# A hybrid decoder block on one core: first branch projection over eight banks, six more slabs in seven products, a shorter recurrence on VectorE

## The chip, the cores and the metric

The kernel runs on one core of a Trainium2 chip. What counts is the device time of one execution in microseconds. A NeuronCore has TensorE (PE in the profile, its weight loads PEld), VectorE (DVE), ScalarE (ACT), GpSimd (POOL) and SyncE (SP), which issues most of the loads. Each engine works through its own queue in order; the engines wait for each other by semaphores. TensorE writes into PSUM, eight banks of 128 x 512 float32 numbers here.

## The reference

One block of a decoder on 512 tokens of width 1024, with 16 meta tokens ahead (T = 528), in float32. Cut to what matters here:

```python
u = rmsnorm(h, mix_norm_w)
q, k, v, g_ret, lru_in, lru_gate, gate_a, gate_b = split(u @ w_in)      # eight times 1024 columns
o = chunk_retention(rotary(q), rotary(k) * dk ** -0.5, v)               # 8 heads, chunks of 128
y_ret = (silu(g_ret) * headnorm(o)) @ w_branch_ret
c = causal_depthwise_conv(lru_in, conv_w, conv_b)                       # 4 taps
r = sigmoid(c @ wa + ba); i = sigmoid(c @ wx + bx)                      # 4 blocks of 256
log_a = -8 * r * softplus(-lam); a = exp(log_a)
h_t = a_t * h_{t-1} + sqrt(-expm1(2 * log_a)) * (i * c)                 # the recurrence
y_lru = (gelu(lru_gate) * hs) @ w_branch_lru
h = h + (sigmoid(gate_a) * y_ret + sigmoid(gate_b) * y_lru) @ w_out
h = h + swiglu(rmsnorm(h, ffn_norm_w))                                  # hidden 2816
return rmsnorm(h, final_norm_w)[:, 16:]
```

## The kernel before

**Products.** Every float32 operand is split in two parts, `hi` (rounded to float32r by ScalarE, line 358) and `lo` (the rest, by VectorE, line 364). A product is three matmuls: hi x hi, hi x lo, lo x hi. The text counts matmuls as products where it counts TensorE's instructions.

**Slabs.** `w_in` is worked in 32 slabs of 256 columns, by their first letters: Q, K, G (retention), I (`lru_in`), L (`lru_gate`), A (`gate_a`), B (`gate_b`), four of each. A slab's weight is a 2 x 2 matrix of quarters (`a11`, `a12`, `a21`, `a22`, each 128 x 512), multiplied with the 2 x 2 matrix of blocks of u (`b11` to `b22`, 512 rows and 256 tokens, 264 with half the meta tokens). *Plain* (`plain`, `plain512`) it takes eight block products of twelve matmuls, 96. *Fast* (`fast`, `fast512`, `fast528`) it is Strassen's scheme in Winograd's form: seven block products, 84 matmuls. That needs sums of quarters (`s1` to `s4`, made by `combine` on VectorE, line 283, or for a next fast slab's `s1` by an accumulating load on GpSimd's queue), the differences `t1` to `t4` of u's blocks, held in the dictionary U, and a longer eviction: `pz`, `ws`, `u2` collect partial sums of four banks or half banks z, w, y, x, and two additions write the result. `plain_slab` says which slabs are plain: K0, G0, I2, I3, all L and all B; the gates of A and most of Q, K, G, I0 and I1 are fast.

**Pieces and their ring.** `emit` makes the pieces in the order of `pieces`, which follows PLAN: load a quarter, combine if needed, cast, subtract. A plain slab has four pieces of 128 x 512, a fast one seven. `hi` and `lo` have nine buffers each (RING), the raw quarters eight, the sums three.

**Steps.** PLAN lists the steps: R0 to R3 (queries, keys, values, retention gates; the heads' work is dealt out in small pieces behind later products by `defer` and `tick`), A (sigmoid gates of the first branch), I (`lru_in` and the convolution), BR (`branch`: `w_branch_ret`, two halves of four banks, each half running over all eight row tiles of 128; a source's split parts are held from the first half to the second), T (the recurrent gates of a block and, deferred, `recurrence`), L (`lru_gate`), B, BL (second branch, `branch` too, with `merged`). The step BR gives back the buffers of t1 to t4 first, BL those of the four blocks.

**Recurrence.** With t = tanh(4 softplus r) and e = exp(-8 softplus r) from ScalarE, six instructions a half block on VectorE and one on GpSimd: d = (e + 1) t, d = (e - 1) + d, d = (e + 1) d, a = -d / 2 + e, u = (a + 1) sqrt(t), GpSimd's product with i c (line 1241), the scan. GpSimd also makes i c itself (line 1215, 128 x 1056).

**Order.** The queues are not in the written order: except for the first steps, a scheduler with a timeline of its own sorts the instructions of each engine when the program is built. It lets TensorE change between open accumulations where a piece or a bank comes late. Work buffers come from 32 slots of 128 x 1056 float32 (`Slots`).

Of the kernel before, what the change touches and what calls it, by code (L numbers as in the profile page):

```python
# [17 lines left out]
P = 128  # L18
D = 1024
# [48 lines left out]
FIRST_LOADS = "w1 w2 w3 x1 w4 w5 w6 w7 r2 m r3 r0 r1"  # L68


PLAN = "R0 R1 R2 R3 A0 A1 A2 A3 I0 I1 BR T0 L0 I2 T1 L1 I3 L2 T2 B0 L3 T3 B1 B2 B3 BL"

PLAIN_R = "K0 G0".split()
NORM, LAST_NORM = 2.0, 3.7
SUM = 2.0

# [39 lines left out]
class Slots:  # L116
# [12 lines left out]
    def get(self, n=SEQ, dt=F32):  # L129
        if n <= T and dt == F32:  # L130
            if self.halves:
                slot, i = self.halves.pop(0)
            else:
                slot, i = [*self.open(dt), 0], 0
                self.halves.append((slot, 1))
            slot[2] += 1
            t = slot[1][:, i * T:i * T + n]
            self.held[id(t)] = (t, slot, i)
        else:
            tag, mem = self.open(dt)  # L140
            t = mem[:, :n]
            self.held[id(t)] = (t, tag, None)
        return t

    def put(self, *tiles):
        for t in tiles:
            _, slot, i = self.held.pop(id(t))
            if i is None:
                self.free.append(slot)
                continue  # L150
            slot[2] -= 1
            self.halves.append((slot, i))
# [6 lines left out]
def hybrid_block(ctx: ExitStack, tc: tile.TileContext, a: dict):  # L159
# [10 lines left out]
    def bank(name):  # L170
        return ps.tile([P, 512], F32, tag="ps", name=name)
# [48 lines left out]

    def plain_slab(key, i):
        if key == "w_in":
            return i in [{"Q": Q, "K": K, "G": G}[r[0]] + int(r[1]) for r in PLAIN_R] or LI + 2 <= i < GA or i >= GB
        return key == "w_fi" and i < FIRST

    pieces = []
    for n, (key, i) in enumerate(order):
        if n == 0:
            pieces += PLAIN_V
        if key in ("w_br", "w_bl"):  # L230

            pieces += [(key, k // 2, k % 2 + 2 * (1 - i)) for k in range(KT)]
        elif plain_slab(key, i):
            pieces += [(key, i, c) for c in PLAIN]
        elif key == "w_v":
            pieces += [(key, j, c) for c in FAST for j in (i, i + 1)] if i else []
        elif key in ("w_in", "w_fi"):
            pieces += [(key, i, c) for c in FAST]
        elif key == "w_fo":
            pass  # L240
        else:
            pieces += [(key, i, c) for c in range(2 if key == "gates" else 4)]
# [153 lines left out]
    def lookup(*args, **kw):  # L396
        state["table"] = behind(nc.scalar.activation(*args, **kw), state.get("table"))
# [39 lines left out]
    def mm3(out, wh, wl, xh, xl, start, stop):  # L437

        nc.tensor.matmul(out, wh, xh, start=start, stop=False, skip_group_check=True)  # L439
        nc.tensor.matmul(out, wh, xl, start=False, stop=False, skip_group_check=True)  # L440
        nc.tensor.matmul(out, wl, xh, start=False, stop=stop, skip_group_check=True)  # L441
        tick(3 * out.shape[-1] / 2400)
# [766 lines left out]
    def recurrence(group):  # L1209
        two = lambda t: t.rearrange("p (j t) -> p j t", j=2)  # L1210


        A = {}
        for b, r, g, c in group:
            nc.gpsimd.tensor_tensor(g, g, c, op=ALU.mult)
            put(c)
            A[b] = get(2 * T)
            a3, r3 = two(A[b]), two(r)
            for j in range(2):
                k = 2 * b + j  # L1220
                lookup(a3[:, j], r3[:, j], AF.Exp, scale=spm8[:, k:k + 1])
                lookup(r3[:, j], r3[:, j], AF.Tanh, scale=sp4[:, k:k + 1])
        yield STEPS[0]
        ds = {}
        for b, r, g, c in group:
            for j in range(2):
                a, t = two(A[b])[:, j], two(r)[:, j]
                d = ds[b, j] = get(T)
                nc.vector.scalar_tensor_tensor(d, a, 1.0, t, ALU.add, ALU.mult)
                lookup(t, t, AF.Sqrt)  # L1230
                nc.vector.scalar_tensor_tensor(d, a, 1.0, d, ALU.subtract, ALU.add)
            yield STEPS[1]
        for b, r, g, c in group:
            for j in range(2):
                a, t, d, g1 = two(A[b])[:, j], two(r)[:, j], ds[b, j], two(g)[:, j]
                nc.vector.scalar_tensor_tensor(d, a, 1.0, d, ALU.add, ALU.mult)
                nc.vector.scalar_tensor_tensor(a, d, -0.5, a, ALU.mult, ALU.add)
                put(d)
                yield STEPS[2]
                nc.vector.scalar_tensor_tensor(t, a, 1.0, t, ALU.add, ALU.mult)  # L1240
                nc.gpsimd.tensor_tensor(g1, g1, t, op=ALU.mult)
                yield STEPS[3]
                nc.vector.tensor_tensor_scan(t, a, g1, 0.0, ALU.mult, ALU.add)
            put(A[b], g)
            while Z[b] is None:
                yield 0.5
            z3 = two(Z[b])
            (nc.gpsimd if Z_POOL else nc.vector).tensor_tensor(z3, z3, two(r)[:, :, NM:], op=ALU.mult)
            put(r)
            ready.add(b)  # L1250

    def lru_gate(s):
        x = get(D)
        for j, pb in enumerate(plain512(LG + s, "lg")):
            lookup(x[:, j * SEQ:(j + 1) * SEQ], pb, AF.Gelu_apprx_tanh)
        Z[s] = x


# [22 lines left out]
    for step in plan:  # L1281
        s = int(step[1]) if step[1:2].isdigit() else None
        if step[0] == "R":
            ret_project(s)
            if s == 0:
                softplus()
            if s == 3:
                put(ropef)
        elif step == "BR":
            for i in range(4):  # L1290
                retained(i)
            for b in ("t1", "t2", "t3", "t4"):
                put(*U.pop(b))
            branch("w_br", lambda i: R[i], gated(macc, GA))
        elif step == "BL":
            for b in ("b11", "b12", "b21", "b22"):
                put(*U.pop(b))
            branch("w_bl", recurred, merged)
        elif step[0] == "A":
            gate(s, GA)  # L1300
        elif step[0] == "B":
            gate(s, GB)
        else:
            {"I": lru_in, "T": lru_gates, "L": lru_gate}[step[0]](*(int(i) for i in step[1:]))
# [325 lines left out]
```

## Time and profile before

| what | us |
|---|---|
| median of three runs | 901.25 (900.97 to 901.37) |
| the profiled execution's own time | 901.45 |
| its span, first to last instruction | 899.7 |
| VectorE busy in the span | 709.8 |
| ScalarE busy in the span | 500.2 |
| GpSimd busy in the span | 118.7 |

The profile gives, for one execution, every instruction with its start, duration and what ended its engine's wait. By the first matmuls of each step: the A gates start at 207.3 us, I0 and I1 fill about 260 to 288 with the first products of BR among them, BR ends at 328.9, T0 to B3 run from there to 466.5, BL to 510.7, the output projection to about 558, the FFN's first product to 787 and its second to the end. A matmul's recorded duration includes its way through the array, so the durations of neighbours overlap, and the distance between starts is what one costs. The granted TensorE clock is 0.998 of full speed over the span.

### The profile page before, as it was taken

The numbers are of one execution on the slowest core, as the hardware profiler recorded it, in microseconds if no ns is written. First come the engines' busy times: TensorE is split into PE (matmuls) and PEld (weight loads), VectorE is DVE, ScalarE is ACT, GpSimd is POOL, SyncE is SP. The second block draws the span as 40 slices with busy tenths as digits, with TensorE's granted clock in tenths as the row PEclk, the third lists the DMA queues.
The fourth block names the chain that finished last, engine by engine and source line by source line (L and its number), as shares of the span: only waits on it lengthen the run. The fifth ranks groups of instructions, "written<-read, shape, count | busy, mean of one in ns | idle before, by whom it ended". The sixth has DMA issues, their size and how long they took to land.

```text
span 899.7 us, 17038 instructions
## 1 busy us (share of the span) xinstructions
PE 888.5 (99%) x6470; PEld 841.4 (94%) x6470; DVE 709.8 (79%) x1164; ACT 500.2 (56%) x938; POOL 118.7 (13%) x154
## 2 busy tenths in 40 slices
PE   8999999999999999999999999999999999999996
PEld 7999999999999889999998888999999999988885
DVE  5998897999788738868745526989989998899973
ACT  6655655656556246857833315555556555665653
POOL 3202311212110011211200211000000000111112
PEclk9999999999999999999999999999999999999999
DMA  9734244445354333233442232133333335685622
GB/s 321 210 126 107 72 138 124 115 135 135 87 151 140 105 95 94 71 115 97 142 137 88 92 93 70 61 106 116 99 117 94 116 101 146 179 234 141 141 47 93
DMA packets 58145, 109.11 MB, mean 121 GB/s; under 512 B 6592, under 2 KB 6848, under 8 KB 58064
## 3 DMA queue, kind: packets, MB, share of 16 engines
q1 hardware_dynamic: 51152, 94.37, 33.0%
q0 software_dynamic: 5328, 9.70, 6.7%
q10 hardware_dynamic: 1584, 3.97, 1.4%
q8 instruction: 50, 0.82, 0.4%
q14 instruction: 31, 0.25, 0.1%
HBM read 105.92 MB, written 2.10 MB: 120 GB/s over the span
## 4 chain that ended last, share of the span: by engine, by line
PE 97%; DVE 1%; DMA 1%; ACT 1%; issue 0%; POOL 0%; POOLq 0%; ACTq 0%; DVEq 0%
PE zwf L449 4%; PE zwf L451 4%; PE zwf L450 4%; PE fo L441 4%; PE fo L440 4%; PE fo L439 4%; PE yxf L450 3%; PE yxf L449 3%; PE yxf L451 3%; PE gate L451 2%; PE lg L451 2%; PE lg L450 2%; PE gate L449 2%; PE gate L450 2%; PE lg L449 2%; PE wo L441 2%
## 5 line engine op out<-in xcount | busy, mean ns | idle before, releaser
L364 DVE TENSOR_TENSOR lo<-raw_w_in,hi 128x512 fp32r<-128x512 f32 x96 | 68.3, 718 | 28.5 <-ACT hi L358 26.3
L451 PE MATMUL zwf<-b,lo 128*128 128x256 f32 x320 | 90.2, 282 | 0.0
L449 PE MATMUL zwf<-b,hi 128*128 128x256 f32 x320 | 90.0, 282 | 0.0
L450 PE MATMUL zwf<-b,hi 128*128 128x256 f32 x320 | 90.0, 281 | 0.0
L358 ACT CAST hi<-raw_w_in 128x512 fp32r<-128x512 f32 x96 | 59.0, 620 | 50.0 <-PE w_br L440 13.9
L358 ACT CAST hi<-s_w_fi 128x512 fp32r<-128x512 f32 x80 | 49.7, 621 | 50.8 <-PE zwf L450 36.7
L450 PE MATMUL yxf<-b,hi 128*128 128x256 f32 x240 | 67.5, 281 | 0.0
L449 PE MATMUL yxf<-b,hi 128*128 128x256 f32 x240 | 67.4, 281 | 0.0
L451 PE MATMUL yxf<-b,lo 128*128 128x256 f32 x240 | 66.6, 281 | 0.0
L364 DVE TENSOR_TENSOR lo<-s_w_fi,hi 128x512 fp32r<-128x512 f32 x80 | 54.9, 687 | 13.5 <-ACT hi L358 13.5
L358 ACT CAST hi<-s_w_in 128x512 fp32r<-128x512 f32 x64 | 39.7, 623 | 42.7 <-PE zwgate L450 9.2
L358 ACT CAST hi<-raw_w_fi 128x512 fp32r<-128x512 f32 x68 | 41.9, 621 | 34.6 <-PE yxf L450 19.4
L450 PEld LDWEIGHTS zwf<-b,hi 128*128 128x128 f32 x320 | 60.6, 189 | 0.0
L449 PEld LDWEIGHTS zwf<-b,hi 128*128 128x128 f32 x320 | 60.5, 189 | 0.0
L451 PEld LDWEIGHTS zwf<-b,lo 128*128 128x128 f32 x320 | 60.5, 189 | 0.0
L440 PE MATMUL fo<-lo,b 128*128 128x512 f32 x158 | 59.1, 394 | 0.0
L439 PE MATMUL fo<-hi,b 128*128 128x512 f32 x158 | 57.5, 393 | 0.0
L441 PE MATMUL fo<-hi,b 128*128 128x512 f32 x158 | 56.1, 394 | 0.0
L505 ACT CAST b<-b 128x512 fp32r<-128x512 f32 (+3 forms) x58 | 39.2, 689 | 26.7 <-DVE b L1176 11.6
L506 DVE TENSOR_TENSOR b<-b,b 128x512 fp32r<-128x512 f32 (+3 forms) x58 | 48.7, 849 | 3.4 <-ACT b L505 3.3
L364 DVE TENSOR_TENSOR lo<-s_w_in,hi 128x512 fp32r<-128x512 f32 x64 | 43.5, 685 | 7.7 <-ACT hi L358 7.2
L364 DVE TENSOR_TENSOR lo<-raw_w_fi,hi 128x512 fp32r<-128x512 f32 x68 | 46.4, 685 | 3.9 <-ACT hi L358 3.3
(438 smaller groups left out, 3182.8 us busy)
## 6 DMA issues: line engine op xcount, KB each, us to landing
raw_w_in<-in_w_in SPq DMA_DIRECT2D x112, 256.0 KB, 3.2
raw_w_fi<-in_w_fi SPq DMA_DIRECT2D x86, 256.0 KB, 3.1
raw_w_fo<-in_w_fo SPq DMA_DIRECT2D x44, 256.0 KB, 4.0
raw_w_br<-in_w_br SPq DMA_DIRECT2D x16, 256.0 KB, 3.1
raw_w_bl<-in_w_bl SPq DMA_DIRECT2D x16, 256.0 KB, 3.5
raw_w_out<-in_w_out SPq DMA_DIRECT2D x16, 256.0 KB, 2.9
raw_w_v<-in_w_v SPq DMA_DIRECT2D x15, 256.0 KB, 5.5
s_w_in<-in_w_in SPq DMA_DIRECT2D x15, 256.0 KB, 3.4
```

Source lines behind the costliest of these rows:

```text
L358: highs.append(nc.scalar.copy(hi, src))
L364: return engine.tensor_tensor(lo, src, hi.bitcast(F32), op=ALU.subtract)
L439: nc.tensor.matmul(out, wh, xh, start=start, stop=False, skip_group_check=True)
L440: nc.tensor.matmul(out, wh, xl, start=False, stop=False, skip_group_check=True)
L441: nc.tensor.matmul(out, wl, xh, start=False, stop=stop, skip_group_check=True)
L449: nc.tensor.matmul(out, wh, xh, start=start and i == 0, stop=False, skip_group_check=True)
L450: nc.tensor.matmul(out, wh, xl, start=False, stop=False, skip_group_check=True)
L451: nc.tensor.matmul(out, wl, xh, start=False, stop=i == 3, skip_group_check=True)
L505: high = nc.scalar.copy(hi, src)
L506: low = engine.tensor_tensor(lo, src, hi.bitcast(F32), op=ALU.subtract)
```

## The change

Five edits.

1. **BR in eight banks.** `whole_branch` opens all eight banks of `w_br` and runs once over the eight row tiles. Each source R[i] (two tiles) is split, used for both halves at once, and its parts are given back; for the last source the products are grouped by bank, so that bank after bank is finished and evicted.
2. **PLAN.** BR stands ahead of I1, T2 ahead of L2, B0 behind T3.
3. **Fast slabs.** I2, L1 and B0 to B3 become fast; plain are I3, L0, L2, L3 (and K0, G0). `lru_gate` gets the fast path.
4. **Differences kept.** t1 to t4 stay in U until BL.
5. **Recurrence.** a = 1 - d with d = (e + 1) t takes the place of three instructions, and the two products on GpSimd (i c, and that with u) are made on VectorE. Per half block VectorE now has d, a, u, the product and the scan.

```diff
-PLAN = "R0 R1 R2 R3 A0 A1 A2 A3 I0 I1 BR T0 L0 I2 T1 L1 I3 L2 T2 B0 L3 T3 B1 B2 B3 BL"
+PLAN = "R0 R1 R2 R3 A0 A1 A2 A3 I0 BR I1 T0 L0 I2 T1 L1 I3 T2 L2 L3 T3 B0 B1 B2 B3 BL"
+PLAIN_L = "I3 L0 L2 L3".split()
...
-            return i in [{"Q": Q, "K": K, "G": G}[r[0]] + int(r[1]) for r in PLAIN_R] or LI + 2 <= i < GA or i >= GB
+            first = {"Q": Q, "K": K, "G": G, "I": LI, "L": LG, "B": GB}
+            return i in [first[r[0]] + int(r[1]) for r in PLAIN_R + PLAIN_L]
...
+        if key == "w_br":
+            pieces += [(key, k // 2, k % 2 + 2 * (1 - hf)) for k in range(KT) for hf in range(2)] if i == 0 else []
...
+    def whole_branch(key, source, done):
+        parts = {}
+        acc = [bank(f"{key}{c}") for c in range(KT)]
+        def product(c, k, w):
+            x = [p[:, k % 2 * SEQ:(k % 2 + 1) * SEQ] for p in parts[k // 2]]
+            mm3(acc[c], *(p[:, c % 4 * P:(c % 4 + 1) * P] for p in w), *x, k == 0, k == KT - 1)
+        for i in range(4):
+            f = source(i)
+            parts[i] = get(D, F32R), get(D, F32R)
+            split(parts[i], f)
+            put(f)
...
+            if i < 3:
+                for k, hf in names:
+                    w = weights(pieces_of[k, hf])[0]
+                    for c in range(4):
+                        product(4 * hf + c, k, w)
+            else:
+                ws = dict(zip(names, weights(*pieces_of.values())))
+                for c in range(KT):
+                    for k in (2 * i, 2 * i + 1):
+                        product(c, k, ws[k, c // 4])
+                    done(c, acc[c])
+            put(*parts.pop(i))
...
-            nc.gpsimd.tensor_tensor(g, g, c, op=ALU.mult)
+            nc.vector.tensor_tensor(g, g, c, op=ALU.mult)
...
                 nc.vector.scalar_tensor_tensor(d, a, 1.0, t, ALU.add, ALU.mult)
                 lookup(t, t, AF.Sqrt)
-                nc.vector.scalar_tensor_tensor(d, a, 1.0, d, ALU.subtract, ALU.add)
+                nc.vector.tensor_scalar(a, d, -1.0, 1.0, ALU.mult, ALU.add)
...
-                nc.vector.scalar_tensor_tensor(d, a, 1.0, d, ALU.add, ALU.mult)
-                nc.vector.scalar_tensor_tensor(a, d, -0.5, a, ALU.mult, ALU.add)
...
                 nc.vector.scalar_tensor_tensor(t, a, 1.0, t, ALU.add, ALU.mult)
-                nc.gpsimd.tensor_tensor(g1, g1, t, op=ALU.mult)
+                nc.vector.tensor_tensor(g1, g1, t, op=ALU.mult)
...
-            for b in ("t1", "t2", "t3", "t4"):
-                put(*U.pop(b))
-            branch("w_br", lambda i: R[i], gated(macc, GA))
+            whole_branch("w_br", lambda i: R[i], gated(macc, GA))
...
-            for b in ("b11", "b12", "b21", "b22"):
+            for b in list(U):
```

What the scheduler makes of it shows at three places; a name's last number is that of its buffer, and lines of the changed kernel are three higher for the same helper (442 for 439, 452 for 449, 367 for 364). On TensorE, the start of BR before: the last matmuls of I1's seventh product (`xli17`), then one bank after another of the first half (`w_br0_0`, `w_br0_1`).

```order
L449 MATMUL xli17_3851<-b7_113,hi138_3751 128x264
L450 MATMUL xli17_3851<-b8_114,hi138_3751 128x264
L451 MATMUL xli17_3851<-b7_113,lo138_3752 128x264
L439 MATMUL w_br0_0_4008<-b90_4012,hi142_3822 128x512
L440 MATMUL w_br0_0_4008<-b91_4013,hi142_3822 128x512
L441 MATMUL w_br0_0_4008<-b90_4012,lo142_3823 128x512
L439 MATMUL w_br0_1_4009<-b90_4012,hi142_3822 128x512
```

The start of BR in the change, a few matmuls behind I0's last: `w_br0` to `w_br7` are the eight banks, `hi137` and `hi138` are the weights of the second row tile (columns 0 to 511 and 512 to 1023), `hi139` is one of the third tile, `hi136` that of the first tile's second columns.

```order
L442 MATMUL w_br3_3850<-b86_3855,hi137_3729 128x512
L443 MATMUL w_br3_3850<-b87_3856,hi137_3729 128x512
L444 MATMUL w_br3_3850<-b86_3855,lo137_3730 128x512
L442 MATMUL w_br4_3851<-b86_3855,hi138_3747 128x512
L443 MATMUL w_br4_3851<-b87_3856,hi138_3747 128x512
L444 MATMUL w_br4_3851<-b86_3855,lo138_3748 128x512
L442 MATMUL w_br0_3847<-b91_3946,hi139_3765 128x512
L443 MATMUL w_br0_3847<-b92_3947,hi139_3765 128x512
L444 MATMUL w_br0_3847<-b91_3946,lo139_3766 128x512
L442 MATMUL w_br1_3848<-b91_3946,hi139_3765 128x512
L443 MATMUL w_br1_3848<-b92_3947,hi139_3765 128x512
L442 MATMUL w_br5_3852<-b86_3855,hi136_3711 128x512
```

TensorE goes on with the second and third row tile in banks 0 to 4 before the first tile reaches bank 5: 27 matmuls stand between I0's last one and the first in bank 5.

On VectorE, the recurrence of block 3 before: the instructions on lines 1229, 1231, 1236, 1237 and 1240 with `lo` of the plain slabs B2 and B3 among them (`w_in31` is B3).

```order
L1229 SCALAR_TENSOR_TENSOR b134_5688<-b133_5665,b130_5580 128x528
L1231 SCALAR_TENSOR_TENSOR b134_5688<-b133_5665,b134_5688 128x528
L364 TENSOR_TENSOR lo203_5701<-raw_w_in31_3_5698,hi203_5700 128x512
L1236 SCALAR_TENSOR_TENSOR b134_5688<-b133_5665,b134_5688 128x528
L1229 SCALAR_TENSOR_TENSOR b134_5688<-b133_5665,b130_5580 128x528
L1237 SCALAR_TENSOR_TENSOR b133_5665<-b134_5688,b133_5665 128x528
L364 TENSOR_TENSOR lo204_5735<-raw_w_in31_0_5732,hi204_5734 128x512
L1231 SCALAR_TENSOR_TENSOR b134_5688<-b133_5665,b134_5688 128x528
L1240 SCALAR_TENSOR_TENSOR b130_5580<-b133_5665,b130_5580 128x528
L1236 SCALAR_TENSOR_TENSOR b134_5688<-b133_5665,b134_5688 128x528
L364 TENSOR_TENSOR lo205_5768<-raw_w_in31_1_5765,hi205_5767 128x512
L1237 SCALAR_TENSOR_TENSOR b133_5665<-b134_5688,b133_5665 128x528
```

The same place in the change: lines 1261 (d), 1263 (a), 1269 (u), 1270 (the product that was GpSimd's), with `lo` of B1 and, on line 477, B0's partial sum `pz`.

```order
L1261 SCALAR_TENSOR_TENSOR b136_5610<-b135_5583,b132_5484 128x528
L1263 TENSOR_SCALAR b135_5583<-b136_5610 128x528
L367 TENSOR_TENSOR lo206_5622<-raw_w_in29_2_5559,hi206_5621 128x512
L477 TENSOR_TENSOR pzgate28_5554<-zwgate28_5551,wsgate28_5553 128x256
L1261 SCALAR_TENSOR_TENSOR b137_5614<-b135_5583,b132_5484 128x528
L1269 SCALAR_TENSOR_TENSOR b132_5484<-b135_5583,b132_5484 128x528
L1263 TENSOR_SCALAR b135_5583<-b137_5614 128x528
L367 TENSOR_TENSOR lo207_5638<-s4_w_in29_5569,hi207_5637 128x512
L1270 TENSOR_TENSOR b133_5485<-b133_5485,b132_5484 128x528
L367 TENSOR_TENSOR lo208_5661<-raw_w_in29_1_5658,hi208_5660 128x512
L1269 SCALAR_TENSOR_TENSOR b132_5484<-b135_5583,b132_5484 128x528
L286 TENSOR_TENSOR s2_w_in30_5704<-s1_w_in30_5556,raw_w_in30_2_5698 128x512
```

Three of the five instructions a half are one now, the product has come to this queue, and what stands between them belongs to seven-product slabs.

On TensorE, where B3 and BL meet, before: the last plain product of B3 (`gate31_1`), then BL's first banks.

```order
L449 MATMUL gate31_1_5928<-b13_119,hi205_5767 128x256
L450 MATMUL gate31_1_5928<-b14_120,hi205_5767 128x256
L451 MATMUL gate31_1_5928<-b13_119,lo205_5768 128x256
L439 MATMUL w_bl0_0_6051<-b137_6055,hi206_5806 128x512
L440 MATMUL w_bl0_0_6051<-b138_6056,hi206_5806 128x512
L441 MATMUL w_bl0_0_6051<-b137_6055,lo206_5807 128x512
L439 MATMUL w_bl0_1_6052<-b137_6055,hi206_5806 128x512
```

In the change, 23 matmuls of BL (`w_bl0_0` to `w_bl0_3`) stand ahead of B3's fifth to seventh product (`zwgate31` with `hi221`, then `yxgate31`):

```order
L443 MATMUL w_bl0_2_6141<-b142_6144,hi225_6008 128x512
L444 MATMUL w_bl0_2_6141<-b141_6143,lo225_6009 128x512
L442 MATMUL w_bl0_3_6142<-b141_6143,hi225_6008 128x512
L443 MATMUL w_bl0_3_6142<-b142_6144,hi225_6008 128x512
L452 MATMUL zwgate31_6001<-b13_119,hi221_5925 128x256
L453 MATMUL zwgate31_6001<-b14_120,hi221_5925 128x256
L454 MATMUL zwgate31_6001<-b13_119,lo221_5926 128x256
```

The scheduler has put BL's first products in front of those that need B3's sum `s4`.

More of the change, by code (lines that the diff above doesn't have):

```diff
@@ L229, in hybrid_block @@
             pieces += PLAIN_V
-        if key in ("w_br", "w_bl"):
+        if key == "w_br":
+            pieces += [(key, k // 2, k % 2 + 2 * (1 - hf)) for k in range(KT) for hf in range(2)] if i == 0 else []
+        elif key == "w_bl":
             pieces += [(key, k // 2, k % 2 + 2 * (1 - i)) for k in range(KT)]
@@ L558, in branch @@
                 done(4 * hf + c, acc[c])
+    def whole_branch(key, source, done):
[9 more added lines that the diff above has]
+            put(f)
+            names = [(k, hf) for k in (2 * i, 2 * i + 1) for hf in range(2)]
+            pieces_of = {(k, hf): (key, i, k % 2 + 2 * (1 - hf)) for k, hf in names}
+            if i < 3:
[10 more added lines that the diff above has]
+            put(*parts.pop(i))
     def rsqrt_mean(ssq, count, w, name, parts=P, engine=nc.vector):
@@ L1223, in recurrence @@
         yield STEPS[0]
-        ds = {}
         for b, r, g, c in group:
@@ L1227, in recurrence @@
                 a, t = two(A[b])[:, j], two(r)[:, j]
-                d = ds[b, j] = get(T)
+                d = get(T)
                 nc.vector.scalar_tensor_tensor(d, a, 1.0, t, ALU.add, ALU.mult)
                 lookup(t, t, AF.Sqrt)
-                nc.vector.scalar_tensor_tensor(d, a, 1.0, d, ALU.subtract, ALU.add)
+                nc.vector.tensor_scalar(a, d, -1.0, 1.0, ALU.mult, ALU.add)
+                put(d)
             yield STEPS[1]
@@ L1234, in recurrence @@
             for j in range(2):
[L1235 to L1239, printed above, removed]
+                a, t, g1 = two(A[b])[:, j], two(r)[:, j], two(g)[:, j]
                 nc.vector.scalar_tensor_tensor(t, a, 1.0, t, ALU.add, ALU.mult)
-                nc.gpsimd.tensor_tensor(g1, g1, t, op=ALU.mult)
+                nc.vector.tensor_tensor(g1, g1, t, op=ALU.mult)
                 yield STEPS[3]
@@ L1253, in lru_gate @@
         x = get(D)
-        for j, pb in enumerate(plain512(LG + s, "lg")):
-            lookup(x[:, j * SEQ:(j + 1) * SEQ], pb, AF.Gelu_apprx_tanh)
+        if plain_slab("w_in", LG + s):
+            for j, pb in enumerate(plain512(LG + s, "lg")):
+                lookup(x[:, j * SEQ:(j + 1) * SEQ], pb, AF.Gelu_apprx_tanh)
+        else:
+            fast512("w_in", LG + s, UV, x, "lg")
+            lookup(x, x, AF.Gelu_apprx_tanh)
         Z[s] = x
```

## The prediction

> **What bounds the kernel now.** The page first: span, engines, chain of waits.
>
> ```profile
> span 899.7 us, 17038 instructions
> PE 888.5 (99%) x6470; PEld 841.4 (94%) x6470; DVE 709.8 (79%) x1164; ACT 500.2 (56%) x938; POOL 118.7 (13%) x154
> PE 97%; DVE 1%; DMA 1%; ACT 1%; issue 0%; POOL 0%; POOLq 0%; ACTq 0%; DVEq 0%
> ```
>
> TensorE is busy for 888.5 of 899.7 us and holds 97% of the chain. A share alone says little, so the windows next. From the left: stretch and its length, then busy time and instructions of PE, PEld, DVE, ACT, POOL, and the granted clock.
>
> ```profile
> 260.00:280.00 20.00, 20.00 (x168) 20.00 (x167) 14.28 (x29) 13.28 (x24) 0.86 (x1) 1.00 0.56 156
> 280.00:329.00 49.00, 49.00 (x235) 40.96 (x234) 34.08 (x58) 15.48 (x28) 0.00 (x0) 1.00 0.35 110
> 329.00:466.00 137.00, 137.00 (x1150) 137.00 (x1149) 98.50 (x134) 93.36 (x152) 24.04 (x12) 1.00 0.34 108
> 210.00:260.00 50.00, 50.00 (x431) 50.00 (x430) 42.57 (x83) 29.13 (x76) 9.75 (x10) 1.00 0.41 113
> 585.00:700.00 115.00, 115.00 (x972) 115.00 (x971) 105.29 (x174) 65.50 (x127) 0.00 (x0) 1.00 0.35 108
> ```
>
> The changed steps lie in the first three rows (I0 and I1; BR with I1's end; T0 to B3). TensorE has no idle time in any of them, and its clock is whole. The last two rows are stages of seven-product slabs that exist already: VectorE is busy there for 85% (42.57 of 50) and 92% (105.29 of 115), and TensorE still waits for nothing. So a product taken out of these stretches is time taken off, until VectorE or ScalarE delivers late. The forecast needs two sums: what TensorE is spared, and whether VectorE can keep up with the rest.
>
> **What TensorE is spared.** A plain slab is 96 products, a seven-product slab 84. Six slabs change (I2, L1, B0 to B3); the instruction order has 72 products fewer and nothing else missing on TensorE. Recorded durations overlap, so the price is the distance of starts:
>
> ```profile
> L449 PE MATMUL lg<-b,hi x32: 278/280/283, 386.6 to 397.6; 128*128 128x256 f32 x32
> L449 PE MATMUL li<-b,hi x32: 279/282/286, 374.9 to 386.2; 128*128 128x264 f32 x32
> ```
>
> Between the first and last start of one line lie 31 x 3 products: 11.0 / 93 = 0.1183 us at 256 columns, 11.3 / 93 = 0.1215 us at 264. The saving is 60 x 0.1183 + 12 x 0.1215 = **8.56 us**. BR has its 192 products of 512 columns in either form: nothing. The Trainium skill (TensorE: Matmul & The Clock Gate, "Back-to-back issue gap") puts a warm matmul at N / 2.4 + 2.5 ns, 109 ns at 256 columns; by it the saving would be 7.9 us. The rows here are 8% slower than the page, and the rows decide.
>
> **What VectorE is given.** First its prices: in the stretch T0 to B3, then in the A gates.
>
> ```profile
> L364 DVE TENSOR_TENSOR lo<-raw_w_in,hi 128x512 fp32r<-128x512 f32 x34 | 26.4, 780 | 12.9 <-ACT hi L358 12.9
> L1243 DVE TENSOR_TENSOR_SCAN b<-b,b 128x528 f32<-128x528 f32 x8 | 10.0, 1249 | 3.6 <-POOL b L1241 3.6
> L506 DVE TENSOR_TENSOR b<-b,b 128x1024 fp32r<-128x1024 f32 x4 | 7.1, 1786 | 1.1 <-ACT b L505 1.1
> L1231 DVE SCALAR_TENSOR_TENSOR b<-b,b 128x528 f32<-128x528 f32 x8 | 5.6, 703 | 0.1
> L1236 DVE SCALAR_TENSOR_TENSOR b<-b,b 128x528 f32<-128x528 f32 x8 | 5.6, 700 | 0.0
> L1237 DVE SCALAR_TENSOR_TENSOR b<-b,b 128x528 f32<-128x528 f32 x8 | 5.6, 697 | 0.0
> L1176 DVE SCALAR_TENSOR_TENSOR b<-b,vec,b 128x525 f32<-128x525 f32 x4 | 5.3, 1314 | 0.0
> L1176 DVE SCALAR_TENSOR_TENSOR b<-b,vec,b 128x527 f32<-128x527 f32 x4 | 3.1, 768 | 0.1
> L1248 DVE TENSOR_TENSOR b<-b,b 128x1024 f32<-128x1024 f32 x4 | 4.9, 1219 | 0.1
> L506 DVE TENSOR_TENSOR b<-b,b 128x528 fp32r<-128x528 f32 x4 | 2.8, 708 | 2.0 <-ACT b L505 2.0
> L1174 DVE TENSOR_SCALAR b<-b,vec 128x528 f32<-128x528 f32 x4 | 2.2, 554 | 0.1
> ```
>
> ```profile
> L364 DVE TENSOR_TENSOR lo<-raw_w_in,hi 128x512 fp32r<-128x512 f32 x13 | 8.8, 685 | 0.7 <-ACT hi L358 0.5
> L283 DVE TENSOR_TENSOR s_w_in<-raw_w_in,raw_w_in 128x512 f32<-128x512 f32 x4 | 2.7, 686 | 0.1
> L491 DVE TENSOR_TENSOR b<-yxgate,pzgate 128x512 f32<-128x512 f32 x3 | 2.0, 682 | 0.0
> L474 DVE TENSOR_TENSOR pzgate<-zwgate,wsgate 128x256 f32<-128x256 f32 x4 | 1.7, 415 | 0.0
> L506 DVE TENSOR_TENSOR b<-b,b 128x1024 fp32r<-128x1024 f32 x1 | 1.2, 1211 | 0.0
> L812 DVE TENSOR_TENSOR b<-b,b 128x1056 f32<-128x1056 f32 x1 | 1.2, 1246 | 0.0
> ```
>
> Two things have to be read out of these before they are multiplied. Durations overlap here too, and some are stretched by GpSimd:
>
> ```profile
> 413.37 0.70 DVE L1231 SCALAR_TENSOR_TENSOR b<-b,b 128x528 f32<-128x528 f32 x1
> 413.99 0.70 DVE L1240 SCALAR_TENSOR_TENSOR b<-b,b 128x528 f32<-128x528 f32 x1
> 404.51 1.29 DVE L364 TENSOR_TENSOR lo<-raw_gates,hi 128x512 fp32r<-128x512 f32 x1 [1.58 <-ACT hi L358]
> 402.67 2.59 POOL L1215 TENSOR_TENSOR b<-b,b 128x1056 f32<-128x1056 f32 x1 [19.02 <-ACT b L397]
> ```
>
> The next instruction starts 0.62 us after one that is recorded with 0.70: each costs 0.08 us less than its record. And the lo of 404.51 took 1.29 us where one alone takes 0.685: it ran into GpSimd's product, which ended at 405.26. GpSimd's 24.04 us in the 137 us window are these products, and they go. In the means, the excess is 34 x 0.095 (lo), 4 x 0.57 (splits of 1024) and 4 x 0.55 (the 525 form, which stands beside 768 for 527): 7.7 us that VectorE gets back.
>
> The Trainium skill (SBUF — State Buffer, "Who interferes with whom") says that VectorE and GpSimd share a pair of ports which is locked for a whole instruction, so the later comer is blocked outright. The record above agrees: that lo ended 0.54 us after GpSimd did. By that rule up to all 24 us could come back, by the means 7.7; neither alters TensorE's sum.
>
> Edits on VectorE, each price less 0.08. **Six slabs**: 18 lo and 19 combinations more, 37 x 0.606 = 22.4 us; evictions for five of 256 columns (0.335 + 2 x 0.60) and I2 some 9.5 us. **Recurrence**: 24 three-operand instructions out (0.62 each), 8 scalar ones (0.474), 8 products of 528 (0.62) and 4 of 1056 (1.166) in: -14.9 + 3.8 + 5.0 + 4.7 = -1.4 us. The products have no row of their own on VectorE; the split of 528 (708 ns) and the 1056 form of L812 are the same kind and size, bounds 0.5 to 0.8. So DVE's total should go from 709.8 to about 732 us.
>
> Can it keep up? From I1's end to B3's last lo the new order has 181 rows on VectorE. By record: 72 lo and combinations 49.4; three convolutions with splits 21.4; four recurrences 41.0; evictions 10.7; two splits of Z 2.4; together 124.9, less 181 x 0.08 = **110.4 us**. TensorE needs 372 x 0.1215 + 708 x 0.1183 = **129.0 us** there. That is 86%, between the 85% and 92% that stall nothing above. Locally it is tighter. B0 to B3 last 336 x 0.1183 = 39.8 us; VectorE owes four times (10 x 0.606 + 1.54) = 30.4, block 3's recurrence 9.2 and two Z splits 2.3: 41.9, so 2.1 over. The ring of nine pieces, 9 x 12 x 0.1183 = 12.8 us of lead, has to carry it, and BL behind has room.
>
> ```profile
> DVE b L1229 <- ACT b L397: 8.2, 4, 2.7
> L397 ACT ACT_TABLE_LOAD x17 | 21.8, 1283 | 0.3
> L358 ACT CAST hi<-raw_w_in 128x512 fp32r<-128x512 f32 x34 | 20.7, 618 | 11.9 <-PE li L450 7.7 <-PE w_br L440 2.1 <-PE lg L450 1.7
> L482 ACT COPY u2li<-xli 128x264 f32<-128x264 f32 x2 | 0.7, 371 | 0.0
> L1155 DVE TENSOR_TENSOR b<-xli,pzli 128x256 f32<-128x256 f32 x2 | 0.8, 414 | 0.0
> raw_w_br<-in_w_br SPq DMA_DIRECT2D x16, 256.0 KB, 3.1
> ```
>
> A recurrence also waits on ScalarE's table loads: 8.2 us in four waits, the longest 2.7, with lo's queued behind it. Hence the **stall in B0 to B3**: at best 0 (the ring hides all), at worst 2.1 + 2.7 = 4.8 us. I take 1.3, nearer to the two stages that show none, but not nothing: B3's second piece gets its ring slot only when B1's last products are done, 28 products (3.3 us) before it is due, and a cast (0.62), a Z split (1.13) and its own lo (0.61) stand in between, with whatever VectorE is behind by then.
>
> ScalarE gets 18 more casts (0.62) and some 15 copies (0.37), while ten lookups of 512 become five of 1024: 93.4 + 16.7 = 110 of 129 us, 85%. It stays behind VectorE, and its casts wait for ring slots that TensorE frees, not the other way round.
>
> **The moved steps.** BR goes ahead of I1, and with it 16 loads on SyncE's queue ahead of I1's; one lands in 3.1 us (last row above) while 12 products of 512 columns use it, so the queue has slack: 0. What BR reads is ready: the last heads' transposes stand ahead of I0 in both orders. I1's convolution loses BR as its cover and now lies beside T0 and L0; T2 goes ahead of L2 and B0 behind T3, which puts four seven-product slabs in a row. Both are in the two sums above, and the second is why B0 to B3 carry the charge.
>
> **BR.** It now needs eight banks while I0's four are not evicted. A copy (0.37) and four evictions (0.41 each) take 2.0 us; the order covers them with 27 products of 512 columns on five banks. The four source splits are due over 192 products, not over the first 96. I take 0; if the cover fails, up to 2.0 us. Keeping the differences U adds nothing on an engine; it holds eight of the 32 work buffers until BL, and a buffer that came free late would delay its first writer. No wait of before is on one; I take 0, at worst one eviction (0.6 us). The five additional accumulating loads on GpSimd's queue replace its products; 0, since DMA is at 0.34 of its time there.
>
> **Sum.** The profiled execution took 901.45 us (span 899.7): 901.45 - 8.56 + 1.3 = 894.2. It lies 0.2 above the median of 901.25, so for the median **894.0 us**.
>
> **Rivals.** *The ring hides everything*: 892.7. For it: 86% over the whole stretch. Against: 2.1 us over locally. *VectorE sets the pace in B0 to B3*: the full 4.8, 897.5. For it: the seven-product slabs stand four in a row with a recurrence among them; the A gates had a retention tail there, at 85%. *BR waits for banks*: 894.0 + 2.0 = 896.0. The Trainium skill (Perfetto Trace Analysis, "Matmuls") wants groups to rotate through banks so that one is emptied while the next fills, which eight at once give up; no row of before shows such a wait. *Slower*: every recurrence holds VectorE's queue at a table load as long as the longest wait, 2.7 us, with too little lead: 4 x 2.7 = 10.8, 901.25 - 8.56 + 10.8 = 903.5. It decides from 2.1 us per block on (8.56 / 4). Against: around T0 to T2 stand plain slabs, whose piece feeds 24 products (2.84 us), so that the ring's lead is up to twice that of B0 to B3. *The gain is lost again* by a mix of these: near 901. That the change does not do what it says is out as far as TensorE's products go.
>
> **Chances.** Forecast (893 to 895) 0.48, all hidden 0.2, banks 0.1, VectorE's pace 0.12, lost again 0.06, slower 0.04. The range runs from all hidden to the full stall with a little over, 892.4 to 898.2; 0.1 lies outside above, little below. Within 0.2% (1.8 us, about what a measurement of this kernel can tell from no change) 0.06.
>
> **What would show it.** PE instructions 6398; no wait of TensorE from 330 to the end of T3; if any, some in B0 to B3, released by lo (L364's successor) or by VectorE's partial sums, 1 to 2 us in all; DVE near 732 us; lo means back to 685; POOL near 95 us. Wrong would be: idle TensorE at BR's start, waits at T1 to T3, or gaps in B0 to B3 above 5 us.

## The result and the profile after

| | before | changed |
|---|---|---|
| median, us | 901.31 (4 runs) | 893.92 (893.42 to 894.48, 4 runs) |
| the profiled execution | 901.45 | 894.48 |
| its span | 899.7 | 892.7 |

The ratio is 0.9918, 95% interval 0.9906 to 0.993: faster by 7.4 us. The forecast was 894.0.

The page of the changed kernel, with the same three lines as before: span, engines, chain of waits by engine.

```profile
span 892.7 us, 17031 instructions
PE 880.9 (99%) x6398; PEld 832.6 (93%) x6398; DVE 728.3 (82%) x1217; ACT 511.8 (57%) x964; POOL 100.0 (11%) x147
PE 96%; DVE 1%; issue 1%; ACT 1%; DMA 1%; POOL 0%; POOLq 0%; ACTq 0%; DVEq 0%
```

TensorE has 72 instructions fewer and is busy 7.6 us less, which is the whole difference of the spans (7.0) and a little more. VectorE works 18.5 us more, GpSimd 18.7 less. The windows (stretch and length, busy time of PE, PEld, DVE, ACT, POOL, granted clock, DMA share, GB/s): I0 with BR's start, BR and then I1, T0 to B3, and two stretches within the last.

```profile
260.00:280.00 20.00, 20.00 (x149) 19.14 (x149) 11.83 (x26) 10.50 (x20) 0.00 (x0) 1.00 0.52 155
280.00:329.00 49.00, 49.00 (x249) 41.56 (x248) 30.85 (x49) 14.94 (x25) 0.86 (x1) 1.00 0.35 108
329.00:459.00 130.00, 129.92 (x1071) 129.03 (x1071) 119.55 (x196) 105.37 (x181) 4.32 (x5) 1.00 0.41 122
363.00:390.00 27.00, 27.00 (x226) 27.00 (x226) 25.54 (x43) 23.11 (x41) 0.00 (x0) 1.00 0.38 125
419.00:460.00 41.00, 40.92 (x325) 39.87 (x324) 37.68 (x58) 32.63 (x56) 2.59 (x3) 1.00 0.58 167
```

Of 137 us from T0 to B3, 130 are left, and TensorE is still busy in all but 0.08 of them. VectorE went from 72% (98.50 of 137) to 92%, in places 95% (25.54 of 27), and TensorE waits for it nowhere that the table of TensorE's waits lists. By the starts of matmuls there is one pause, 0.35 us at 438.6 among the B slabs, behind ScalarE's copy of a partial sum. VectorE's groups and its own waits from 326 to 460 us:

```profile
L367 DVE TENSOR_TENSOR lo<-raw_w_in,hi 128x512 fp32r<-128x512 f32 x31 | 21.0, 684 | 3.2 <-ACT hi L361 3.2
L367 DVE TENSOR_TENSOR lo<-s_w_in,hi 128x512 fp32r<-128x512 f32 x24 | 16.3, 686 | 3.5 <-ACT hi L361 2.7 <-PE gt L444 0.8
L1272 DVE TENSOR_TENSOR_SCAN b<-b,b 128x528 f32<-128x528 f32 x8 | 10.0, 1249 | 0.0
L1270 DVE TENSOR_TENSOR b<-b,b 128x528 f32<-128x528 f32 x8 | 5.6, 694 | 0.0
L1248 DVE TENSOR_TENSOR b<-b,b 128x1056 f32<-128x1056 f32 x4 | 5.0, 1250 | 0.0
L509 DVE TENSOR_TENSOR b<-b,b 128x1024 fp32r<-128x1024 f32 x4 | 4.9, 1219 | 0.1
L1263 DVE TENSOR_SCALAR b<-b 128x528 f32<-128x528 f32 x8 | 3.4, 429 | 0.1
```

```profile
DVE b L1269 <- ACT b L400: 3.5, 3, 1.2
DVE b L1261 <- ACT b L400: 1.4, 1, 1.4
```

The `lo` of 780 ns is back at 684 to 686, the split of 1786 at 1219, and the scan no longer waits for GpSimd. The wait on ScalarE's table loads fell from 8.2 to 4.9 us.

Where the 7 us went, by summed distances from each matmul's start to the next, grouped by the name of the bank, which needs no model of a matmul's end:

| group | before | changed | difference |
|---|---|---|---|
| gates of A and B | 85.88 | 80.68 | -5.20 (0.35 of pauses included) |
| L slabs | 45.43 | 44.06 | -1.37 |
| I slabs | 43.63 | 42.31 | -1.32 |
| BR, BL | 44.06, 44.22 | 44.42, 44.58 | +0.36, +0.36 |
| start of the program (warm-up, values; to 41 us) | 30.22 | 30.91 | +0.69 |
| output projection and FFN | 376.34 | 375.72 | -0.62 |
| all others | | | -0.1 |
| from the last matmul's start to the end of the span | 7.67 | 7.88 | +0.2 |

### The profile page after: what moved, and what is told of

Read it like the earlier page. It is cut to its first block, busy times and chain, and to the rows that moved or that the text cites. A ratio compares the mean times of both kernels' runs of the same rounds, so it can differ in the third digit from the quotient of the medians.

```text
span 892.7 us, 17031 instructions
## 1 busy us (share of the span) xinstructions
PE 880.9 (99%) x6398; PEld 832.6 (93%) x6398; DVE 728.3 (82%) x1217; ACT 511.8 (57%) x964; POOL 100.0 (11%) x147
## 4 chain that ended last, share of the span: by engine, by line
PE 96%; DVE 1%; issue 1%; ACT 1%; DMA 1%; POOL 0%; POOLq 0%; ACTq 0%; DVEq 0%
PE zwf L453 4%; PE zwf L454 4%; PE zwf L452 4%; PE fo L443 4%; PE fo L444 4%; PE fo L442 4%; PE yxf L452 3%; PE yxf L454 3%; PE yxf L453 3%; PE w_bl L442 2%; PE wo L444 2%; PE wo L443 2%; PE w_bl L443 2%; PE w_br L442 2%; PE w_br L444 2%; PE w_bl L444 2%
## 5 line engine op out<-in xcount | busy, mean ns | idle before, releaser
L361 ACT CAST hi<-s_w_in 128x512 fp32r<-128x512 f32 x88 | 54.4, 621 | 58.0 <-PE w_br L443 6.5
L361 ACT CAST hi<-raw_w_in 128x512 fp32r<-128x512 f32 x90 | 55.5, 620 | 43.1 <-PE w_br L443 8.5
L367 DVE TENSOR_TENSOR lo<-s_w_in,hi 128x512 fp32r<-128x512 f32 x88 | 59.8, 686 | 17.4 <-ACT hi L361 16.3
L367 DVE TENSOR_TENSOR lo<-raw_w_in,hi 128x512 fp32r<-128x512 f32 x90 | 60.8, 684 | 10.8 <-ACT hi L361 10.6
L509 DVE TENSOR_TENSOR b<-b,b 128x512 fp32r<-128x512 f32 (+3 forms) x58 | 46.4, 809 | 1.0 <-ACT b L508 0.9
L452 PEld LDWEIGHTS yxf<-b,hi 128*128 128x128 f32 x240 | 45.3, 189 | 0.0
```

What stands on the lines that cost most here:

```text
L361: highs.append(nc.scalar.copy(hi, src))
L367: return engine.tensor_tensor(lo, src, hi.bitcast(F32), op=ALU.subtract)
L452: nc.tensor.matmul(out, wh, xh, start=start and i == 0, stop=False, skip_group_check=True)
L509: low = engine.tensor_tensor(lo, src, hi.bitcast(F32), op=ALU.subtract)
```

## The experiments

All are the changed kernel with the edit shown. Times are medians; the kernel before ran beside each and took 901.2 to 901.4 us. The queues are sorted anew for every kernel, so an edit can move other instructions too.

**1. The products alone.** All six slabs plain again; order, BR, differences and recurrence stay as changed.

```diff
-PLAIN_L = "I3 L0 L2 L3".split()
+PLAIN_L = "I2 I3 L0 L1 L2 L3 B0 B1 B2 B3".split()
```

> All edits of the change but the third: I2, L1 and B0 to B3 stay plain (96 products each). Theory, TensorE's product count carries the whole gain: by the changed kernel's own distances of starts the six slabs cost 7.9 us less in seven products (gates 5.2, L1 1.4, I2 1.3), so this takes 893.9 + 7.9 = 901.8 us, 901.0 to 902.6, level with before. Rival, BR in eight banks, the new PLAN or the recurrence carry part of it: below 900.5 us.

902.15 us (901.8 to 902.43) beside 901.34: ratio 1.0008 (0.9998 to 1.0017). The window T0 to B3 of this kernel:

```profile
329.00:464.00 135.00, 135.00 (x1133) 135.00 (x1132) 92.78 (x143) 92.73 (x153) 0.00 (x0) 1.00 0.33 103
```

VectorE has only 92.78 us of work in 135, and nothing is won by it: without fewer products, the four other edits are worth nothing (0.8 us to the worse, at the limit of what can be told). The six slabs make 902.15 - 893.92 = 8.2 us, and 902.15 lies where the theory had it (901.0 to 902.6). What the other edits are for has to be asked with the fast slabs in place.

**2 and 12. BR over two halves again.**

```diff
-        if key == "w_br":
-            pieces += [(key, k // 2, k % 2 + 2 * (1 - hf)) for k in range(KT) for hf in range(2)] if i == 0 else []
-        elif key == "w_bl":
+        if key in ("w_br", "w_bl"):
...
-            whole_branch("w_br", lambda i: R[i], gated(macc, GA))
+            branch("w_br", lambda i: R[i], gated(macc, GA))
```

> The change with BR as before, two halves of four banks each, at its new place. Theory: BR's 192 products are the same and neither form makes TensorE wait, so 893.9 us within 0.7. Rival, eight banks save or cost a wait at BR's start or end: off by more than 1 us, with gaps of TensorE between 270 and 320 us.

893.1 us (892.79 to 893.28), and BR took 44.38 us by starts where the changed kernel has 44.42, with no pause in either. So eight banks neither cost nor give anything in BR. But the median was 0.8 lower, so both kernels ran again side by side:

> The changed kernel itself, beside the next one on the same chip: 893.9 +- 0.6.

> The changed kernel with the right branch's products again over two halves of four banks, as before the change. It gave 893.1 where the changed kernel gave 893.9. Theory (eight banks neither cost nor gain, the difference was the start of the program, which varies between executions): within 0.5 us of the changed kernel in this comparison, and a right branch of 44.3 to 44.5 us in the profile. Rival (the two halves are really the better, by how ScalarE and VectorE share their evictions): 0.6 to 1.0 us below it in most rounds.

The changed kernel took 893.68 (893.35 to 893.87), the two halves 892.86 (892.8 to 893.32). That is 0.8 us again, and neither pair's ranges overlap: the rival held. It is the best version of this study (ratio to before 0.9907, 0.989 to 0.9923). It is not BR that is shorter, though. Matched start by start, the two profiled executions stand within 0.15 us of each other up to 629 us, then the two halves gain 0.37 us in the FFN's first product (629 to 793). What that product has to do with BR's form wasn't tried; it stays open, as does the other half of the difference.

**3, 5 and 6. The recurrence.** Three kernels make a table of two edits: the identity, and the engine of the two products.

```diff
-            nc.vector.tensor_tensor(g, g, c, op=ALU.mult)
+            nc.gpsimd.tensor_tensor(g, g, c, op=ALU.mult)
...
-                nc.vector.tensor_tensor(g1, g1, t, op=ALU.mult)
+                nc.gpsimd.tensor_tensor(g1, g1, t, op=ALU.mult)
```

```diff
-                nc.vector.tensor_scalar(a, d, -1.0, 1.0, ALU.mult, ALU.add)
...
+                nc.vector.scalar_tensor_tensor(d, a, 1.0, d, ALU.subtract, ALU.add)
...
+                nc.vector.scalar_tensor_tensor(d, a, 1.0, d, ALU.add, ALU.mult)
+                nc.vector.scalar_tensor_tensor(a, d, -0.5, a, ALU.mult, ALU.add)
...
```

The first diff alone is run 3, both are run 5, the second alone is run 6.

> The change with the recurrence's two products back on GpSimd, the shorter identity kept. Theory, VectorE's room is needed but not used up: VectorE is spared 9.6 us of its own and loses some 7.7 us to instructions that GpSimd stretches, its busy time from 329 to 460 us stays near 119 us, lo means rise to about 0.78 us; at most 1.5 us of TensorE's waits, 893.5 to 895.5 us. Rival, moving the products was what made room for the slabs: 896.5 us or more.

> The change with the whole old recurrence: the longer identity, and the two products on GpSimd. Theory, VectorE's time decides once it passes some 92% of the stretch from T0 to B3: against the run with the products alone on GpSimd (899.3 us) it owes 24 x 0.62 - 8 x 0.35 = 12 us more and has no room left, so 8 to 11 us more of TensorE's waits: 907 to 911 us, slower than before by about 1%. Rival, what hurt there was only where GpSimd's products fell, and the identity is hidden: 899 to 901 us.

> The change with the longer identity, all of it and both products on VectorE. Theory, VectorE's time decides: 12 us more than in the change, 132 us of work from 329 to 460 us against 129 us of TensorE; some 4 to 8 us of waits, 898 to 902 us. Rival, only GpSimd's stretching of VectorE's instructions hurts: 894 to 895.5 us.

| | products on VectorE | products on GpSimd |
|---|---|---|
| short identity | 893.92 (the change) | 899.32 (899.0 to 899.61) |
| long identity | 895.23 (894.62 to 895.41) | 901.91 (901.66 to 902.5) |

So the engine of the products is worth 5.4 to 6.7 us and the identity 1.3 to 2.6. Run 3's theory missed (it gave 893.5 to 895.5), so did run 5's (907 to 911, too slow) and run 6's (898 to 902, too slow). The rivals of runs 3 and 6 held, that of run 5 (899 to 901) missed by 0.9. What is wrong with GpSimd shows in run 3: TensorE's waits, then VectorE's and GpSimd's groups from I1's end to B3.

```profile
PE zli L452 <- DVE pzli L477: 1.3, 1, 1.3
PE zwgate L454 <- DVE lo L367: 1.1, 2, 0.7
PE gt L442 <- DVE b L1197: 0.8, 1, 0.8
```

```profile
L367 DVE TENSOR_TENSOR lo<-s_w_in,hi 128x512 fp32r<-128x512 f32 x24 | 20.5, 869 | 3.6 <-ACT hi L361 3.6
L1272 DVE TENSOR_TENSOR_SCAN b<-b,b 128x528 f32<-128x528 f32 x8 | 13.3, 1666 | 1.2 <-POOL b L1270 1.2
L1270 POOL TENSOR_TENSOR b<-b,b 128x528 f32<-128x528 f32 x8 | 14.3, 1796 | 43.6 <-DVE b L1269 42.3 <-ACT hi L361 1.3
```

The `lo` goes from 686 to 869 ns and the scan from 1249 to 1666, and TensorE waits at seven places, mostly for VectorE's results, for a little each time. In run 5 one such place shows entire: VectorE's `lo` at the head of its queue, GpSimd's product, what TensorE waited for in total, and the window.

```profile
360.96 2.92 DVE L367 TENSOR_TENSOR lo<-raw_w_in,hi 128x512 fp32r<-128x512 f32 x1
```

```profile
360.26 3.08 POOL L1248 TENSOR_TENSOR b<-b,b 128x1056 f32<-128x1056 f32 x1 [3.39 <-ACT b L400]
```

```profile
PE zwlg L452 <- DVE b L1189: 2.8, 1, 2.8
```

```profile
361.00:365.00 4.00, 1.25 (x11) 1.03 (x9) 4.00 (x6) 3.59 (x6) 2.34 (x1) 1.00 0.02 7
```

The `lo` began 0.70 us after GpSimd's product and ended 0.54 us after it (363.88 and 363.34): 2.92 us for 0.685 of work, with the evictions of I2 queued behind it on VectorE and TensorE waiting for their bank. The Trainium skill (SBUF — State Buffer, "Who interferes with whom") calls the pair of ports that the two engines share an exclusive lock for a whole instruction; these rows agree.

Run 6 shows what does not count by itself. Its VectorE is busier than run 3's, and TensorE's waits are these:

```profile
329.00:464.00 135.00, 133.75 (x1098) 132.25 (x1097) 129.31 (x211) 107.41 (x183) 4.31 (x5) 1.00 0.40 113
```

```profile
PE w_bl L442 <- ACT hi L361: 0.6, 1, 0.6
PE zwgate L452 <- ACT b L400: 0.6, 1, 0.6
```

129.31 of 135 us is 96%, more than run 3's 126.35 in the same window, and costs 1.3 us where run 3 costs 5.4. So VectorE's total does not decide between these runs; the rows of run 5 point to how long one of its instructions holds the queue when something due stands behind it.

**9 and 10. Which of the two products.** One each of the first diff's two edits: the first product, i times c, on GpSimd (run 9), or the second, ahead of the scan (run 10).

> As the changed kernel, but the first of the two products of a recurrence (i times c, 128x1056, four of them) goes back to GpSimd; the second stays on VectorE. With both on GpSimd the kernel took 899.3 us, 5.4 over the changed one; the first product there took 4 x 2.76 = 11.0 us of GpSimd's 25.3. Theory (VectorE's instructions are stretched while GpSimd computes, in proportion to that time): 11.0/25.3 of 5.4 = 2.4 us, so 895.5 to 897.0, and the lo splits average 740 to 790 ns. Rival (only the second product hurts, since the scan stands behind it and VectorE waits for it by 1.2 us and the gates after it): at most 894.6, although the lo splits are stretched.

> As the changed kernel, but the second product of a recurrence (128x528, eight of them, right ahead of the scan) goes back to GpSimd; the first stays on VectorE. It took 8 x 1.80 = 14.3 us of GpSimd's 25.3. Theory (stretching in proportion to GpSimd's time): 3.0 us, so 896.3 to 897.8. Rival (this product alone carries the loss, since it stands in the chain to the scan): 898.5 to 900. If both the first and the second run stay below 895, the loss needs both, by a threshold of what VectorE's queue can take before an eviction is late.

Run 9 took 893.97 us (893.65 to 894.94): nothing. Run 10 took 896.31 (895.62 to 896.73): 2.4 us. Both together (run 3) cost 5.4. Run 9's theory missed (895.5 to 897.0) and its rival held; run 10 lies in the range of a theory that run 9 had already shown wrong, and its rival (898.5 to 900) missed. So GpSimd's time is no measure (11 us of it are free), and the parts don't add up. Run 9 blocks single instructions of VectorE as long as ever; two of them and one of GpSimd's:

```profile
361.68 2.71 DVE L1207 TENSOR_SCALAR b<-b,vec 128x528 f32<-128x528 f32 x1
...
389.65 2.69 DVE L1207 TENSOR_SCALAR b<-b,vec 128x528 f32<-128x528 f32 x1
```

```profile
361.19 2.90 POOL L1248 TENSOR_TENSOR b<-b,b 128x1056 f32<-128x1056 f32 x1 [3.99 <-ACT b L400]
```

These are convolutions, 545 ns each in the changed kernel, held for 2.7 us; TensorE waits 0.2 us in all, so what stands behind them is hardly due yet. In run 10 the second product meets the scan and the splits:

```profile
L1272 DVE TENSOR_TENSOR_SCAN b<-b,b 128x528 f32<-128x528 f32 x8 | 12.1, 1526 | 2.1 <-POOL b L1270 2.1
```

```profile
PE zwgate L454 <- DVE lo L367: 1.1, 2, 0.7
```

Its pauses, 2.2 us in four, all lie between 434.7 and 443, among the B slabs, behind block 3's recurrence. There GpSimd's products ran from 428.06 to 429.50 and from 431.35 to 433.06. A `lo` that began at 428.23 took 1.83 us and a scan that began at 431.80 took 2.38, each 1.1 us too long; the two `lo` right behind that scan are those that the pause at 434.7 waits for. In the changed kernel one of them stands ahead of the scan, so the new place has a part in the 2.4 us, and how large it is wasn't told apart. Run 3 has the same four pauses (437.7 to 445.5) and three more at 352 to 391; of these run 9 has one, 0.3 us where run 3 has 1.4, and run 10 none.

**7. The old order.**

```diff
-PLAN = "R0 R1 R2 R3 A0 A1 A2 A3 I0 BR I1 T0 L0 I2 T1 L1 I3 T2 L2 L3 T3 B0 B1 B2 B3 BL"
+PLAN = "R0 R1 R2 R3 A0 A1 A2 A3 I0 I1 BR T0 L0 I2 T1 L1 I3 L2 T2 B0 L3 T3 B1 B2 B3 BL"
```

> The change with the old PLAN: BR behind I1, L2 ahead of T2, B0 ahead of T3. Theory, the places of the steps matter little as long as VectorE keeps up: 893.9 us within 0.8. Rival, the new places are needed to keep VectorE ahead: 895.5 us or more, with waits of TensorE in T1 to B3.

898.98 us (898.65 to 900.5): the theory missed, the new places are worth 5.1 us. But the wait is in BR, not from T1 to B3 as the rival had it: TensorE's one long wait, ScalarE's queue there (in brackets: how long it waited, and for what), and the windows.

```profile
PE w_br L442 <- ACT b L508: 4.1, 1, 4.1
```

```profile
295.20 1.35 ACT L361 CAST hi<-raw_w_br 128x512 fp32r<-128x512 f32 x2 [3.54 <-PE w_br L443]
296.46 1.57 ACT L508 CAST b<-b 128x1024 fp32r<-128x1024 f32 x2
298.53 1.58 ACT L508 CAST b<-b 128x528 fp32r<-128x528 f32 x2 [0.50 <-DVE b L1209]
```

```profile
295.00:300.00 5.00, 1.09 (x5) 0.56 (x3) 4.36 (x7) 4.19 (x6) 0.00 (x0) 1.00 0.32 103
300.00:304.00 4.00, 3.84 (x10) 3.08 (x11) 2.45 (x2) 0.11 (x1) 0.00 (x0) 0.57 0.02 8
```

TensorE had done one source's 48 products and went on when the last of these casts of L508 ended, at 300.1 (a row puts neighbours together; the last one is 128x1024). It stands on ScalarE behind two casts of weights, the first of which waited 3.54 us for a ring buffer that a product of BR gave back, and behind casts for a convolution (128x528), one of which waited 0.50 us for VectorE. Which of the three moved steps prevents this wasn't tried apart.

**4 and 8. More fast slabs.** All of them (run 4), or L3 alone (run 8).

```diff
-PLAIN_L = "I3 L0 L2 L3".split()
+PLAIN_L = []
```

```diff
-PLAIN_L = "I3 L0 L2 L3".split()
+PLAIN_L = "I3 L0 L2".split()
```

> The change with I3, L0, L2 and L3 in seven products too: 48 products fewer, 5.7 us of TensorE. Theory, VectorE is at 92% from 329 to 460 us and has no room for four more slabs: they ask 4 x 5.3 = 21 us of it, 141 us against 124 of TensorE; BL and the ring take some 6 of the 16 over, the rest stalls TensorE: 893.9 - 5.7 + 10 = 898 us, 895 to 901. Rival, TensorE alone decides: 888.2 us.

> The change with L3 in seven products as well: 12 products fewer, 1.4 us of TensorE. Theory, VectorE has 3.4 us of room from 390 to 419 us and 3.3 from 419 to 460 us and is asked for 5.3 more: most of the 1.4 us is given back, 893 to 895 us. Rival, VectorE has no room at all: 896 us or more; and if it has room enough: 892.5 us.

902.66 us (901.22 to 903.37) and 898.42 (897.46 to 899.39). Forty-eight products fewer cost 8.7 us, twelve fewer 4.5: the change stands at the edge. Both theories gave too little (895 to 901, and 893 to 895); of the rivals only run 8's first held, no room at all. Run 8: TensorE's waits, VectorE at the first of them, and the windows.

```profile
PE gt L442 <- DVE b L494: 3.6, 1, 3.6
PE zwgate L452 <- ACT b L400: 1.6, 1, 1.6
```

```profile
413.63 1.25 DVE L1272 TENSOR_TENSOR_SCAN b<-b,b 128x528 f32<-128x528 f32 x1
...
415.98 1.22 DVE L1277 TENSOR_TENSOR b<-b,b 128x1024 f32<-128x1024 f32 x1
417.11 1.29 DVE L367 TENSOR_TENSOR lo<-s_w_in,hi 128x512 fp32r<-128x512 f32 x2
418.32 0.69 DVE L494 TENSOR_TENSOR b<-yxlg,pzlg 128x512 f32<-128x512 f32 x1
```

```profile
415.00:419.00 4.00, 0.49 (x5) 0.28 (x3) 4.00 (x7) 0.22 (x1) 0.00 (x0) 1.00 0.70 228
419.00:423.00 4.00, 2.30 (x14) 2.00 (x15) 1.20 (x3) 3.35 (x5) 0.86 (x1) 0.69 0.23 70
423.00:427.00 4.00, 4.00 (x21) 4.00 (x21) 2.99 (x4) 3.98 (x9) 0.00 (x0) 0.50 0.39 66
```

T3's gates need a bank that L3's eviction (L494, at 418.32) has yet to free, and that stands on VectorE behind a scan, a sum of quarters, a product of 1024 and three `lo`. A plain slab has a shorter eviction, and twice the products per piece, just where T3 wants banks. Here VectorE's pace does bound, for some 4 us; and waiting costs a second time. After this pause twelve matmuls start at whole clock, 0.12 us apart; then comes the wait of 1.6 us, and behind it TensorE runs at half clock: 21 matmuls in the 4 us from 423, where 226 in 27 us (the changed kernel from 363) make 33, another 1.5 us in this one window.

## Why the prediction was right, point by point

**The sum** (894.0 against 893.92) is right in its main term, and closer than its terms by luck. *72 products*, 8.56 us: the six slabs became 8.4 us shorter without the pauses among them (B0 to B3 5.55, L1 1.38, I2 1.44). The term was mis-sized by 0.2, because it gave a seven-product slab's matmuls the distance of a plain slab's: without the pauses B0 to B3 stand at 118.8 ns, plain at 118.4. The slabs of I that did not change lost another 0.12, so that the table shows 7.89. The Trainium skill's 109 ns (TensorE: Matmul & The Clock Gate, "Back-to-back issue gap"), which gave 7.9 us, agrees only by accident: plain products still stand 118 ns apart, and the page gives the formula for a single matmul by itself. *Stall*, 1.3: 0.35 us was seen, nearer to the rival that the ring hides all. *BR and BL*, 0: each lost 0.36 us, not by pauses but by a pace of 231.4 ns (229.5 before) and 232.2 (230.3), which runs 1 and 2 have too. In run 7, with the old order, BR's pace outside its pause and the half clock behind it is 229.5 again, so in BR it goes with the order; the cause is open. So the sum counted 0.3 too much gain and 0.9 too much stall, and missed 0.7 of slower pace, which nearly cancel. The start of the program, 0.7 longer in this execution, and the output projection and FFN, 0.6 shorter at the same number of products, were not in the sum either and nearly cancel too. The start varies between executions: the profiled ones here and in run 11, of the same kernel, differ by 1.07 us by then.

**Eight banks in BR**, 0 of 2.0: right for BR itself, by run 2 also as an edit of its own; the kernel as a whole is 0.8 us slower by it (runs 2 and 12), in a way that stays open. **Differences kept**, 0: no wait on a buffer is seen; it wasn't run apart.

**VectorE can keep up at 86%**: right in outcome, wrong as a reason. The window shows 92% (119.55 of 130, with six `lo` and two splits for BL in it, which the forecast counted later), the page's total 728.3 where 732 was forecast. Run 6 has 96% and loses 1.3 us; run 3 has 94% and loses 5.4; run 7 has the change's work and loses 5.1, in BR. The argument from shares, 85% and 92% elsewhere, could not have told these apart. The rival with the full stall used the same reason and falls with it; the slower rival (each recurrence holding the queue at a table load) has its mechanism in the trace, 4.9 us of waits in four, but the longest is 1.4 and none reaches TensorE.

**The recurrence**, -1.4 us on VectorE and 7.7 of stretching returned: the prediction took the stretching as a gain in VectorE's time and said that it didn't alter the sum. In fact this is where much of the change's room comes from: with the products on GpSimd (run 3) 5.4 of the 7.4 us are gone. Only the amount was weighed there, not what stands in the queue behind the instruction that is held.

**The moved steps**, taken at 0 for the queues and put into the two sums otherwise: worth 5.1 us (run 7), at BR, where the prediction looked only at loads and banks. It compared what the move costs with what stood before, not with what the rest of the change would cost without it.

**Signs named ahead**: 6398 matmuls, `lo` back at 685, no wait up to the end of T3: as forecast. The wait among the B slabs came to 0.35 us and was released by ScalarE, where 1 to 2 us released by VectorE were named. GpSimd at 100.0, not 95.

## What to carry to other kernels

Where one engine is never idle, products taken out of it are time taken off, priced by the distance of their starts; whether the others keep up is asked at each wait, not by their share of busy time. For an in-order queue, ask which instruction can be held long, and what due work stands behind it: four GpSimd products of 2.8 us, beside convolutions, were free here, and eight of 1.9 us, beside scans and splits, cost 2.4 us. Parts of a change that are worth nothing alone (run 1) may be what makes the rest possible, or may not be needed at all (the eight banks, runs 2 and 12), so undo them one by one from the whole.

## What the hardware showed unexpectedly

A long pause of TensorE cost twice. After 3.7 us (run 8, with the shorter pause behind it) and 4.2 us (run 7) the granted clock stood at 0.50 and 0.57 over windows of 4 us, and after 4.1 us in run 4 likewise:

```profile
421.00:425.00 4.00, 0.15 (x2) 0.00 (x0) 4.00 (x7) 3.97 (x7) 0.00 (x0) 0.94 0.47 166
425.00:429.00 4.00, 3.87 (x18) 3.87 (x19) 3.57 (x5) 3.70 (x10) 0.35 (x1) 0.50 0.22 66
```

After run 5's pause of 2.9 us it stayed at 1.00. The Trainium skill (TensorE: Matmul & The Clock Gate, "Part 1: The HAM clock gate") gives an idle window of about 3.4 us before the clock is halved; these four pauses agree. But one unbroken pause wasn't needed: run 4's clock was at 0.50 from 387 to 390 us as well, behind 4 us in which TensorE was busy for 1.89 and no pause was longer than 1.5 us.

VectorE's instruction beside a GpSimd product was held even where it reads one tensor and scalars for each partition: TENSOR_SCALAR at L1207 took 2.71 us instead of 0.545 (run 9).
